# A hybrid decoder trunk: output projection interleaved with the last attention unit, last FFN sums moved to VectorE, forget gates one tile later

## The chip, the core and the metric

The kernel runs on one core of a Trainium2 chip. That core has a matrix engine (TensorE, PE in the profile; its weight loads are PEld), three engines for elementwise work (VectorE or DVE, ScalarE or ACT, GpSimd or POOL), a queue engine that issues the DMAs (SyncE or SP), an on-chip memory of 128 partitions (SBUF), and an accumulator memory for TensorE's results (PSUM, eight banks of 128x512 f32). The metric is device time in microseconds (us), the lower the better.

## What is computed

Two decoder layers on 1024 tokens of width 1024, all in f32. Layer 0 has sparse attention (compressed, selected and windowed keys, mixed by gates), layer 1 has full attention with forget gates; both add attention into 256 memory tokens, one output projection, and a gated FFN with a causal convolution of width 3. Cut to what matters here:

```python
for l in range(2):
    h = rms_norm(x, attn_norm[l])
    if l == 0:
        o_mix, q_mem = nsa_mixer(h, ...)             # 12 heads: compressed + selected + window
    else:
        hs = rms_norm(x, kv_norm) @ w_kv_shared       # k, v and 12 forget columns
        log_f = log_sigmoid(hs[..., 2 * MIX_W:] + b_fgate)
        dcum = cumsum(log_f, axis=1)                  # enters the scores of layer 1
        o_mix = forgetting_attention(q, k_sh, v_sh, dcum)
    o_mem = memory_attention(q_mem, mem, ...)         # 4 heads
    x = x + concat([o_mix, o_mem]) @ w_o[l]           # the output projection
    x = x + conv_ffn(rms_norm(x, ffn_norm[l]), ...)   # up, conv, silu(a) * b, down
return rms_norm(x, final_norm)
```

## The kernel before

**Arithmetic.** Every f32 product is made of three matmuls of halves: `mm3` (L157, L158, L159) multiplies high by high, high by low and low by high. `split` makes the halves of an operand: ScalarE rounds the high half (L81), VectorE subtracts it from the source (L82).

**Attention** (`attention`). The work is cut into units, one head (`h`) and one half of the tokens (`c`), and each unit into steps `k`. A step transposes a block of probabilities on TensorE (`turn_p`, L399), splits it into `pt` (ScalarE L406, VectorE L409) and two steps later multiplies it by the values (`value`, L422). Scores of later units are begun between the steps (`begin`, L300), masked and maximised on VectorE (L330), exponentiated on ScalarE (L343) and scaled on GpSimd (`normalise`, L366). In layer 0 a unit has a selected part (`ps`), a windowed part (`pw`) and a compressed part (`pc`). A finished unit's result goes through `ob` to DRAM (L515); when both heads of a pair are there, `operand` reads the block back (`wr<-o`, L480), adds the two halves on GpSimd (L481) and splits it into `hT`, the left operand of the output projection. There is one operand for each `c` and each of eight blocks `kt`; block 5 (heads 10 and 11) is the last. At the first step of the last unit the kernel also loads and splits the left half of `w_o` (`load_block`, L190, four pieces of 512 KB through a ring of three `wr` buffers).

**Output projection** (`out_proj`). For each half `n` of the columns and each of eight token tiles `t`, 24 matmuls accumulate in one PSUM bank (`psb`, four banks), with block 5 last; VectorE adds the bank to the residual `x` (L871), which is loaded from DRAM right behind the attention (L1124).

**FFN.** `Up.run` writes out by hand, slot by slot, the order in which VectorE and ScalarE work. `left(k)` makes four sums of two hidden tiles on GpSimd (L1408 to L1411) for the down projection, `store(k)` writes seven tiles of sums to DRAM (`gd`, L1417). `Down.step` multiplies: each step is twelve matmuls; its left operand is read back with `wr<-gd` (`fetch`, L1508), and both operands are split (`prep`) into a ring of four `wh`/`wl` pairs, up to three steps ahead. `sums` (L1529 to L1533) prepares weights on VectorE. `left(10)`, the last, stands behind the first `Down` steps; it writes into `ws` tiles.

**Forget gates.** In `middle`, eight tiles of `layer1_v` (24 matmuls of 390 columns each) are computed in a loop over `t`; the generator `forget` is advanced between them. Its first piece is a chain of small VectorE operations (L994 to L1003), its second multiplies the result by two triangular matrices on TensorE (L1008, L1009), its third transposes and stores (`dd`, L1026).

**Order.** Every engine executes its own queue strictly in order, and all DMAs stand in one queue, SP's. Outside of the stretches that are ordered by hand, a scheduler places the instructions in each queue when the program is built; the places below are read from the built programs.

Of the kernel before, what the change touches and what calls it, by code (L numbers as in the profile page):

```python
# [17 lines left out]
P = 128  # L18
D = 1024
S = 1024  # L20
NT = S // P
KT = D // P
CH = 512
# [6 lines left out]
NF = DFF // P  # L30
# [12 lines left out]
class Trunk:  # L43
# [398 lines left out]
    def attention(self, ap, l, od, units, work, spare, lead=4, lag=2, lead_work=2):  # L442

        units = list(units)
        steps, items, users = [], [], {}
        for k, u in enumerate(units):
            u["start"] = len(steps)
            steps += self.value_steps(u)  # L450
        ends = {id(q[0]): k for k, st in enumerate(steps) for q in st["ps"]}
        for k, u in enumerate(units):
            its, brs = [], u["branches"]
            for br in brs:
                tag, _, bufs = br["p"]
                same = users.setdefault(tag, [])
                br["early"] = ends[id(same[-bufs])] if len(same) >= bufs else -10 ** 9
                same.append(br)
            scored = brs if len(brs) == 1 else brs[0:2]
            for i, br in enumerate(scored):  # L460
                early = max(b["early"] for b in (br, br.get("joint", br)))
                due = next(k for k in range(u["start"], len(steps)) if any(q[0] is br for q in steps[k]["ps"])) - lead
                gs = self.groups(br)
                its += [{"u": u, "br": br, "grp": g, "first": j == 0, "last": g is gs[-1], "early": early, "due": due} for j, g in enumerate(gs)]
                its[-1]["norm"] = (i, len(brs) if br is scored[-1] else i + 1)
            its[0]["load"] = True
            items += its
        self.pace(steps, items)
        n_fill = units[-spare]["start"] if spare else len(steps)
        total, owed, done = sum(n for _, n, _ in work), 0.0, set()  # L470
        work = [[name, gen] for name, _, gen in work]
        later, halves, whole, oT = {}, [], [], []

        def operand():

            if not oT:
                oT.extend(self.hpair() for _ in range(2))
            c, kt = whole.pop(0)
            raw = self.wraw([P, 2, CH])
            self.nc.sync.dma_start(raw, od[c][:, kt * P:(kt + 1) * P, :].rearrange("s p q -> p s q"))  # L480
            self.nc.gpsimd.tensor_tensor(raw[:, 0], raw[:, 0], raw[:, 1], ALU.add)  # L481
            self.split(raw[:, 0], oT[c][0][:, kt, :], oT[c][1][:, kt, :])

        def after(k, slot, f):
            later.setdefault((k, slot), []).append(f)

        def run(k, slot):
            for f in later.pop((k, slot), ()):
                f()

        def advance():
            nonlocal total
            total -= 1
            if next(work[0][1], 0) == 0:
                done.add(work.pop(0)[0])

        def begin(k, it):
            if "load" in it:
                while not set(it["u"]["needs"]) <= done:
                    advance()  # L500
                it["u"]["load"]()
            self.score(it)
            after(k + 1, "max", lambda: self.maximum(ap, it))
            after(k + 1, "exp", lambda: self.exponent(ap, it))
            if "norm" in it:
                after(k + 2, "norm", lambda: self.normalise(ap, it["u"], *it["norm"]))

        def finish(k, u):
            h, c = u["at"]

            def out():
                ot = self.sb(ap, [P, CH], F32, "ob", 2)
                self.nc.scalar.activation(ot, u["o"], AF.Copy)
                for i in range(2):
                    self.nc.sync.dma_start(od[c][i, h * HD:(h + 1) * HD, :], ot[i * HD:(i + 1) * HD, :])  # L515
                halves.append((c, h // 2))
                if halves.count((c, h // 2)) == 2:
                    whole.append((c, h // 2))
            after(k + 1, "exp", out)

        first = min(it["at"] for it in items)
        for k in range(first, len(steps) + lag + 4):
            st = steps[k] if 0 <= k < len(steps) else None
            run(k, "max")
            if st:
                self.turn_p(ap, st)
            run(k, "exp")
            if st:
                self.lower_p(st)
            run(k, "norm")  # L530
            while items and items[0]["at"] <= k:
                begin(k, items.pop(0))
            if k < 0 and lead_work and items:
                for _ in range(lead_work):
                    if work:
                        advance()
            if st and k < n_fill:
                owed += max(total, 0) / (n_fill - k)
                while owed >= 1 and work:
                    owed -= 1  # L540
                    advance()
            if 0 <= k - lag < len(steps):
                self.value(steps[k - lag])
                if steps[k - lag]["end"]:
                    finish(k, steps[k - lag]["u"])
            if not work and whole and k % 4 == 0:
                operand()
            if k == units[-1]["start"]:
                w_o = self.load_block(self.a["w_o"][l], [(0, CH)])
        while whole:  # L550
            operand()
        assert not work and not later
        return oT, w_o

    @staticmethod
    def causal(c, mask):
# [291 lines left out]
    def out_proj(self, l, oT, pool, fx, up):  # L848

        nc, a = self.nc, self.a
        (oT, w), B, late, gb = oT, up.B, [], None
        for n in range(2):
            if n:
                w = self.load_block(a["w_o"][l], [(CH, CH)])
                gb = self.wraw([P, D])
                nc.sync.dma_start(gb, a["ffn_norm"][l:l + 1, :].to_broadcast([P, D]))
                up.load(0)
            for t in range(NT):  # L860
                ps = self.psb()
                oh, ol = oT[t // 4]
                o = (t % 4) * P
                for kt in (0, 1, 2, 3, 4, 6, 7, 5):
                    self.mm3(ps, (oh[:, kt, o:o + P], ol[:, kt, o:o + P]), w(kt, 0, CH), kt == 0, kt == 5)
                if n == 0 and t == NT - 1:
                    up.conv_turn()
                if n and t == NT - 1:
                    up.split_a(0)
                xs = self.x[:, t, n * CH:(n + 1) * CH]  # L870
                nc.vector.tensor_tensor(xs, ps, xs, ALU.add)  # L871
                turns, late = late, self.norm_part(pool, fx, l, t, gb, B) if n else []
                if n and t in (2, 4):
                    (up.sums_21 if t == 2 else up.sums_34)(0)
                if n and t == 1:
                    turns, late = [], turns + late
                for f in turns:
                    f()
        up.load(1)
        up.first(0)  # L880
        up.second(0, True)
        late[0]()
        up.split_a(1)
        up.split_21(0)
        up.first(1)
        for f in late[1:]:
            f()
        up.take_early(0)
        up.second(1, True)
        up.take_early(1)  # L890
        for i in range(4):
            self.turn_split(self.x[:, 4 + i, CH:], B["t3"], i)
            self.turn_split(self.x[:, i, CH:], B["t4"], i)
            if i == 1:
                up.third(0)
                up.split_34(0)
                up.split_b(0)
                up.sums_21(1)
                up.sums_34(1)
# [259 lines left out]
    def middle(self, oT):  # L1159
# [4 lines left out]
        with tc.tile_pool(name="fx0", bufs=1) as fx:  # L1164
            down = self.gated(0, oT, a["x"][0], fx)
            with tc.tile_pool(name="l1v", bufs=1) as vp:
# [25 lines left out]
                with tc.tile_pool(name="l1w", bufs=1) as wp:  # L1192
# [2 lines left out]
                        self.layer1_v(vp, h, 0, t, got["w"], self.psb()[:, 0:390], fb, z)  # L1195
                    forget = self.forget(wp, z)
                    for t in range(NT):
                        if t % 2 == 0:
                            next(forget, None)
                        self.layer1_v(vp, h, 1, t, w1, self.psb()[:, 0:390], fb, z)  # L1200
        return h, got["g"]
# [29 lines left out]
class Up:  # L1231
# [167 lines left out]
    def left(self, k):  # L1399
# [4 lines left out]
        else:  # L1404
            two = [self.k.sb(self.pool, [P, 2, CH], F32, "ws", 2) for _ in range(2)]
            s1, s2, s4 = two[0][:, 0], two[0][:, 1], two[1][:, 0]
        add = self.k.nc.gpsimd.tensor_tensor
        add(s1, g[:, CH:], h[:, CH:], ALU.add)  # L1408
        add(s2, s1, g[:, :CH], ALU.subtract)
        add(g[:, CH:], g[:, :CH], g[:, CH:], ALU.subtract)  # L1410
# [212 lines left out]
```

## Time and profile before

| | |
|---|---|
| time, median of 3 runs (lowest to highest) | 2561.35 us (2555.23 to 2565.48) |
| the profiled execution: its time, its span | 2560.4 us, 2558.4 us |
| granted TensorE clock, mean | 0.993 |
| busy: PE, PEld, DVE, ACT, POOL | 96%, 80%, 73%, 53%, 30% |
| read from and written to HBM | 139 GB/s over the span |

The span goes from the first to the last instruction of the program; what the time has beyond it, 2 us, lies around it. Times in the rows are microseconds from the start of the span. A row of a timeline has the start, the duration, engine, line, operation, tiles and shapes, and in brackets how long the engine had been idle before it and what ended that. In the names of the program's order, the numbers behind a name tell buffers apart; in the profile's rows they are left out.

### The profile page before, as it was taken

The page shows a single profiled execution, that of the slowest core. Times are in us where ns is not written, and L with a number is a line of the kernel's source. Part 1 is how long each engine was busy: PE and PEld are TensorE (multiplying, and loading weights), DVE is VectorE, ACT ScalarE, POOL GpSimd, SP SyncE. Part 2 cuts the span into 40 slices and gives each one's busy share as a digit, 9 for nine tenths or more (in the row PEclk, how much of TensorE's full clock was granted, in tenths as well). Part 3 has the DMA queues.
Part 4 walks back from the last instruction along what each step waited for, and adds up shares of the span by engine and source line. Part 5 has one row for each costly group of instructions (what it writes and reads, how often), then busy time and mean ns, then how long its engine had stood idle before and what let it go on. Part 6 is the DMA issues. An engine that isn't in the chain of part 4 may idle for free.

```text
span 2558.4 us, 35716 instructions
## 1 busy us (share of the span) xinstructions
PE 2460.7 (96%) x12306; PEld 2052.7 (80%) x12306; DVE 1868.4 (73%) x3180; ACT 1345.1 (53%) x2565; POOL 764.1 (30%) x620
## 2 busy tenths in 40 slices
PE   7898999988999999999999999999999999999998
PEld 7787877776878888887888988887777888888787
DVE  5758888887377787777765467878476778878766
ACT  5337777876244454444454356767235444444444
POOL 0104444544034555543000000000234455454000
PEclk9999999999999999999999999999999999999999
DMA  8473234344423333357334466665622233337623
GB/s 251 141 217 113 66 86 116 105 117 131 149 79 102 100 112 99 101 178 280 100 124 149 150 188 189 194 185 169 217 106 86 95 104 111 99 100 263 206 91 123
DMA packets 303276, 357.68 MB, mean 140 GB/s; under 512 B 38024, under 2 KB 183288, under 8 KB 303096
## 3 DMA queue, kind: packets, MB, share of 16 engines
q1 hardware_dynamic: 303096, 355.41, 44.2%
q8 instruction: 97, 1.59, 0.3%
q14 instruction: 83, 0.68, 0.1%
HBM read 245.55 MB, written 109.78 MB: 139 GB/s over the span
## 4 chain that ended last, share of the span: by engine, by line
PE 73%; DVE 8%; ACT 6%; DMA 5%; issue 3%; POOL 3%; SPq 1%; POOLq 0%; ACTq 0%; DVEq 0%
PE psa L157 11%; PE psa L158 11%; PE psa L159 11%; PE psb L157 9%; PE psb L159 9%; PE psb L158 9%; PE psb L399 4%; PE psa L300 4%; PE psb L422 4%; DVE pt L409 2%; POOL ws L1408 2%; ACT pt L406 1%; DMA hT<-in_w_down_dram 1%; DVE ps L330 1%; DVE wl L82 1%
## 5 line engine op out<-in xcount | busy, mean ns | idle before, releaser
L81 ACT ACTIVATE wh<-wr 128x512 fp32r<-128x512 f32 (+2 forms) x254 | 192.7, 763 | 336.4 <-PE psb L159 141.6
L82 DVE TENSOR_TENSOR wl<-wr,wh 128x512 fp32r<-128x512 f32 (+2 forms) x254 | 242.1, 957 | 151.1 <-ACT wh L81 150.4
L1389 DVE SCALAR_TENSOR_TENSOR v<-u,cw,v 128x1023 f32<-128x1023 f32 (+1 forms) x176 | 271.7, 1544 | 69.0 <-ACT v L1387 68.8
L409 DVE TENSOR_TENSOR pt<-psb,pt 128x512 fp32r<-128x512 f32 (+2 forms) x380 | 246.8, 659 | 66.5 <-ACT pt L406 63.4
L1387 ACT ACTIVATE v<-u,cw 128x1024 f32<-128x1024 f32 x88 | 109.6, 1246 | 310.3 <-DVE u L1376 283.6
L406 ACT ACTIVATE pt<-psb 128x512 fp32r<-128x512 f32 (+2 forms) x380 | 213.3, 572 | 87.6 <-PE psb L399 81.3
L422 PE MATMUL psb<-pt,vv 128*128 128x512 f32 (+2 forms) x864 | 225.7, 356 | 18.5 <-DVE pt L409 12.8
L159 PE MATMUL psa<-hT,wl 128*128 128x512 f32 x560 | 218.0, 389 | 0.8 <-DVE wl L82 0.8
L157 PE MATMUL psa<-hT,wh 128*128 128x512 f32 x560 | 218.4, 391 | 0.0
L158 PE MATMUL psa<-hT,wh 128*128 128x512 f32 x560 | 217.9, 389 | 0.0
L300 PE MATMUL psa<-kk,qq 128*128 128x512 f32 (+4 forms) x792 | 184.7, 347 | 13.9 <-DVE stat L330 6.9
L121 POOL TENSOR_TENSOR rs<-ss,consts 128x1 f32<-128x1 f32 x40 | 22.8, 570 | 555.5 <-DVE ss L119 347.5
L422 PEld LDWEIGHTS psb<-pt,vv 128*128 128x128 f32 x864 | 141.0, 191 | 43.9 <-DVE pt L409 21.1
L343 ACT ACTIVATE ps<-ps,stat 128x128 f32<-128x128 f32 (+1 forms) x192 | 147.8, 771 | 46.6 <-DVE stat L330 46.3
L481 POOL TENSOR_TENSOR wr<-wr 128x512 f32<-128x512 f32 x32 | 42.0, 1318 | 428.0 <-ACT pt L406 243.7
L157 PE MATMUL psb<-hT,wh 128*128 128x512 f32 x384 | 156.7, 408 | 1.0 <-DVE pt L409 0.9
L399 PE MATMUL psb<-consts,ps 128*128 128x128 f32 x928 | 148.4, 277 | 8.1 <-DVE pt L409 3.3
L159 PE MATMUL psb<-hT,wl 128*128 128x512 f32 x384 | 151.4, 394 | 0.0
L158 PE MATMUL psb<-hT,wh 128*128 128x512 f32 x384 | 150.7, 393 | 0.0
L330 DVE CUSTOM_DVE_ANT_0 ps<-psa,caub 128x128 f32<-128x128 f32 (+1 forms) x192 | 138.9, 750 | 15.2 <-PE psa L300 14.9
L300 PEld LDWEIGHTS psa<-kk,qq 128*128 128x128 f32 x792 | 120.3, 191 | 30.3 <-DVE stat L330 10.3
L157 PE MATMUL psa<-hx,wh 128*128 128x512 f32 x368 | 144.0, 392 | 0.4 <-ACT u L1379 0.4
(300 smaller groups left out, 6759.3 us busy)
## 6 DMA issues: line engine op xcount, KB each, us to landing
wr<-in_w_up_dram SPq DMA_DIRECT2D x88, 512.0 KB
wr<-gd SPq DMA_DIRECT2D x154, 256.0 KB
gd<-v SPq DMA_DIRECT2D x88, 256.0 KB
o<-ob SPq DMA_DIRECT2D x128, 128.0 KB
wr<-o SPq DMA_DIRECT2D x32, 512.0 KB
hT<-in_w_down_dram SPq DMA_DIRECT2D x64, 256.0 KB
gd<-gs SPq DMA_DIRECT2D x60, 256.0 KB
qd<-st SPq DMA_DIRECT2D x56, 256.0 KB
```

The lines of the kernel that those rows point to most:

```text
L81: nc.scalar.activation(hi, src, AF.Copy)
L82: nc.vector.tensor_tensor(lo, src, f32(hi), ALU.subtract)
L157: mm(out, lh, rh, start=first, stop=False, skip_group_check=more)
L158: mm(out, lh, rl, start=False, stop=False, skip_group_check=more)
L159: mm(out, ll, rh, start=False, stop=last, skip_group_check=more)
L300: nc.tensor.matmul(out, w, rhs, start=b not in banks[:i], stop=b not in banks[i + 1:])
L330: self.nc.vector.tensor_tensor_reduce(p, s, br["spans"][ii][2], -1.0, 3e38, ALU.add, ALU.min, br["stat"][:, 0, ii:ii + 1])
L399: nc.tensor.transpose(tp[0:kb, x:x + P], br["pt"][ii][:, o:o + kb], self.ident)
L406: nc.scalar.activation(st["hi"], st["src"], AF.Copy)
L409: self.nc.vector.tensor_tensor(st["lo"], st["src"], f32(st["hi"]), ALU.subtract)
L422: self.nc.tensor.matmul(out, v, t, start=st["begin"] and i == 0, stop=st["end"] and i == len(mms) - 1)
L1389: nc.vector.scalar_tensor_tensor(v[:, d:], u[:, :S - d], cw[:, tap, i:i + 1], v[:, d:], ALU.mult, ALU.add)
```

## The change

It has three parts.

1. In layer 0 the left half of `w_o` is loaded eight steps earlier (`early`). From the last unit on, when all scores have been begun, each step also issues up to two pieces of the output projection (`ahead`, `out_part`): a piece is three matmuls for one token tile and one block. Seven blocks of the first four token tiles go into four banks of the two `psa` buffers, in the order 0, 1, 2, 3, 6, 4, 7, each as soon as its operand stands in the program's order. `out_proj` then does the seven blocks of tiles 4 and 5, and block 5 of tiles 0 to 5, before tiles 6 and 7. Layer 1 keeps the old way.
2. The four sums of `left(10)`, in both layers, are made on VectorE instead of GpSimd.
3. `forget` is advanced ahead of the tiles 0, 3 and 5 instead of 0, 2, 4 and 6.

```diff
@@ attention
+        early = units[-1]["start"] - 8 if l == 0 else units[-1]["start"]
+        made, rows = set(), {}
...
             self.split(raw[:, 0], oT[c][0][:, kt, :], oT[c][1][:, kt, :])
+            made.add((c, kt))
+
+        def ahead():
+
+            for kt in (0, 1, 2, 3, 6, 4, 7):
+                for t in range(4):
+                    while (0, kt) not in made:
+                        yield
+                    if not rows:
+                        rows.update(enumerate(p[:, x * CH:(x + 1) * CH] for p in (self.psa(), self.psa()) for x in range(2)))
+                    self.out_part(rows[t], oT[0], w_o, t, kt, kt == 0, False)
+                    yield
...
-            if k == units[-1]["start"]:
+            if k == early:
                 w_o = self.load_block(self.a["w_o"][l], [(0, CH)])
+                part = ahead()
+            if l == 0 and k > early + 8 and not items:
+                for _ in range(2):
+                    next(part, None)
         while whole:
             operand()
+        if l == 0:
+            for _ in part:
+                pass
...
+    def out_part(self, ps, oT, w, t, kt, first, last):
+        oh, ol = oT
+        o = (t % 4) * P
+        self.mm3(ps, (oh[:, kt, o:o + P], ol[:, kt, o:o + P]), w(kt, 0, CH), first, last)
@@ out_proj
-            for t in range(NT):
-                ps = self.psb()
...
-                for kt in (0, 1, 2, 3, 4, 6, 7, 5):
+            most = (0, 1, 2, 3, 4, 6, 7)
+            parts = [(t, most + (5,)) for t in range(NT)]
+            if n == 0 and rows:
+                parts = [(t, (5,)) for t in range(4)] + [(4, most), (5, most), (4, (5,)), (5, (5,))] + parts[6:]
+            open_ = dict(rows) if n == 0 else {}
+            for t, kts in parts:
+                ps = open_.setdefault(t, None) or self.psb()
+                open_[t] = ps
+                for kt in kts:
+                    self.out_part(ps, oT[t // 4], w, t, kt, kt == 0, kt == 5)
+                if kts[-1] != 5:
+                    continue
@@ middle
-                        if t % 2 == 0:
+                        if t in (0, 3, 5):
                             next(forget, None)
@@ Up.left
-        add = self.k.nc.gpsimd.tensor_tensor
+        add = (self.k.nc.gpsimd if k < NF // 2 - 1 else self.k.nc.vector).tensor_tensor
```

Three places of the built programs matter below. The first is VectorE's queue shortly before the last unit of layer 0: `wl` is the low half of `w_o`, `hT` an operand of the output projection, `pt` a step's block of probabilities, `stat` the sums of the unit whose `ps` GpSimd scales next (the reciprocal is L355). Before:

```order
L354 TENSOR_SCALAR stat_6814<-stat_6814 128x4
L330 ISA pw_1185_6931,stat_6814<-psa_6923,winb 128x640
L330 ISA stat_6814 128x1
L409 TENSOR_TENSOR pt_6910<-psb_6905,pt_6910 128x512
L355 RECIPROCAL stat_6814<-stat_6814 128x4
L330 ISA pc_6932,stat_6814<-psa_6923,cmpb 128x64
L330 ISA stat_6814 128x1
L82 TENSOR_TENSOR wl_7082<-wr_7079,wh_7081 128x1024
L409 TENSOR_TENSOR pt_6940<-psb_6935,pt_6940 128x512
```

After:

```order
L409 TENSOR_TENSOR pt_6910<-psb_6905,pt_6910 128x512
L82 TENSOR_TENSOR wl_6940<-wr_6937,wh_6939 128x1024
L354 TENSOR_SCALAR stat_6814<-stat_6814 128x4
L82 TENSOR_TENSOR wl_6946<-wr_6943,wh_6945 128x1024
L355 RECIPROCAL stat_6814<-stat_6814 128x4
L82 TENSOR_TENSOR wl_6952<-wr_6949,wh_6951 128x1024
L330 ISA pw_1197_6955,stat_6814<-psa_6923,winb 128x640
L330 ISA stat_6814 128x1
```

Three of the four `wl` now stand together around the reciprocal, and the next step's `pt` (`pt_6964`, in the place of `pt_6940`) stands behind them; further on, `hT_6057<-wr_6971` stands ahead of `pt_7003`, the third block of probabilities from here, where before no operand stood.

The second is GpSimd's queue at the same place: `ps_1163` and the last `pw` are the probabilities of the last unit, `wr` the operands that it adds. Before:

```order
L366 TENSOR_SCALAR ps_1163_6815<-ps_1163_6815,stat_6814,gates 128x1024
L366 TENSOR_SCALAR pw_1185_6931<-pw_1185_6931,stat_6814,gates 128x640 x4
L360 TENSOR_TENSOR stat_6814<-stat_6814,gates 128x4
L481 TENSOR_TENSOR wr_7112<-wr_7112 128x512
L362 TENSOR_TENSOR pc_6932<-pc_6932,stat_6814 128x256
```

After:

```order
L366 TENSOR_SCALAR ps_1163_6815<-ps_1163_6815,stat_6814,gates 128x1024
L483 TENSOR_TENSOR wr_6971<-wr_6971 128x512
L483 TENSOR_TENSOR wr_7051<-wr_7051 128x512
L483 TENSOR_TENSOR wr_7112<-wr_7112 128x512
L483 TENSOR_TENSOR wr_7188<-wr_7188 128x512
L366 TENSOR_SCALAR pw_1197_6955<-pw_1197_6955,stat_6814,gates 128x640 x4
```

Two adds that stood ahead of the last unit's `ps` before, and two that stood behind its `pw`, now stand between them.

The third is VectorE's queue behind `left(10)` in layer 0; each pair of `wl` belongs to one step of `Down`, and L1396 is the slots' work before it. Before:

```order
L1396 TENSOR_TENSOR v_11178<-v_11178,v_11213 128x1024
L82 TENSOR_TENSOR wl_11275<-wr_11102,wh_11274 128x512
L82 TENSOR_TENSOR wl_11275<-hx_10966,wh_11274 128x512
L82 TENSOR_TENSOR wl_11299<-wr_11102,wh_11298 128x512
L82 TENSOR_TENSOR wl_11299<-hx_10966,wh_11298 128x512
```

After:

```order
L82 TENSOR_TENSOR wl_11273<-hx_10964,wh_11272 128x512
L1440 TENSOR_TENSOR ws_11290<-v_11046,v_11176 128x512
L1561 TENSOR_TENSOR hx_11003<-hT_11120 128x512
L1441 TENSOR_TENSOR ws_11290<-ws_11290,v_11046 128x512
L1442 TENSOR_TENSOR v_11046<-v_11046 128x512
L1443 TENSOR_TENSOR ws_11291<-v_11176,ws_11290 128x512
L82 TENSOR_TENSOR wl_11297<-wr_11100,wh_11296 128x512
```

The four sums and one of the weights' sums stand between two steps' pairs.

More of the change, by code (lines that the diff above doesn't have):

```diff
@@ L547, in attention @@
                 operand()
-            if k == units[-1]["start"]:
+            if k == early:
                 w_o = self.load_block(self.a["w_o"][l], [(0, CH)])
+                part = ahead()
+            if l == 0 and k > early + 8 and not items:
+                for _ in range(2):
+                    next(part, None)
         while whole:
             operand()
+        if l == 0:
+            for _ in part:
+                pass
         assert not work and not later
-        return oT, w_o
+        return oT, w_o, rows
+    def out_part(self, ps, oT, w, t, kt, first, last):
+        oh, ol = oT
+        o = (t % 4) * P
+        self.mm3(ps, (oh[:, kt, o:o + P], ol[:, kt, o:o + P]), w(kt, 0, CH), first, last)
     @staticmethod
@@ L852, in out_proj @@
         nc, a = self.nc, self.a
-        (oT, w), B, late, gb = oT, up.B, [], None
+        (oT, w, rows), B, late, gb = oT, up.B, [], None
         for n in range(2):
@@ L859, in out_proj @@
                 up.load(0)
-            for t in range(NT):
-                ps = self.psb()
-                oh, ol = oT[t // 4]
-                o = (t % 4) * P
-                for kt in (0, 1, 2, 3, 4, 6, 7, 5):
-                    self.mm3(ps, (oh[:, kt, o:o + P], ol[:, kt, o:o + P]), w(kt, 0, CH), kt == 0, kt == 5)
+            most = (0, 1, 2, 3, 4, 6, 7)
[10 more added lines that the diff above has]
+                    continue
                 if n == 0 and t == NT - 1:
```

## The prediction

> **What bounds the kernel now.** I read the page's busy times first, then the chain that ended last, then every wait of TensorE over 2 us, then the rows around those that the change touches. The forecast is made against the profiled execution, 2560.4 us (span 2558.4, 2 us around it); the median of the runs, 2561.35, is 0.04% above it.
>
> ```profile
> PE 2460.7 (96%) x12306; PEld 2052.7 (80%) x12306; DVE 1868.4 (73%) x3180; ACT 1345.1 (53%) x2565; POOL 764.1 (30%) x620
> PE 73%; DVE 8%; ACT 6%; DMA 5%; issue 3%; POOL 3%; SPq 1%; POOLq 0%; ACTq 0%; DVEq 0%
> ```
>
> TensorE is busy for 96% of the span and makes up 73% of the chain. The change removes no matmul, so it can only win where TensorE waits, or where its clock drops behind a wait. GpSimd's 3% on the chain is odd for an engine busy 30% of the time, and the chain through layer 0's FFN shows it:
>
> ```profile
> 1166.45 20.27 POOL ws L1408
> 1189.36 0.32 SPq L1417
> 1191.24 3.78 DMA wr<-gd
> 1195.12 1.16 ACT wh L81 x2
> ```
>
> One add of `left(10)` takes 20.27 us; the stores of its sums leave after it; the read-back lies behind them; ScalarE splits what arrives; and TensorE stands still until then. Windows of the stretch (columns: busy time and count of PE, PEld, DVE, ACT, POOL, then granted clock, DMA share, GB/s):
>
> ```profile
> 1140.00:1160.00 20.00, 20.00 (x88) 16.05 (x87) 15.77 (x18) 10.62 (x16) 1.25 (x1) 1.00 1.03 373
> 1160.00:1180.00 20.00, 20.00 (x90) 16.54 (x89) 20.00 (x31) 10.47 (x19) 13.55 (x1) 1.00 0.80 294
> 1180.00:1200.00 20.00, 16.49 (x65) 12.88 (x64) 9.79 (x17) 5.85 (x11) 10.50 (x4) 0.88 0.53 192
> ```
>
> VectorE is busy for all of 1160 to 1180, just where the add crawls. TensorE's rows, layer 0 and then layer 1:
>
> ```profile
> 1191.76 0.39 PE L159 MATMUL psa<-wh,wl 128*128 128x512 f32 x1
> 1192.44 0.39 PE L159 MATMUL psa<-wh,wl 128*128 128x512 f32 x1
> 1196.32 0.79 PE L157 MATMUL psa<-wh 128*128 128x512 f32 x1 [3.49 <-ACT wh L81]
> 1202.33 0.40 PE L158 MATMUL psa<-wl,wh 128*128 128x512 f32 x1
> 2370.12 0.39 PE L159 MATMUL psa<-wh,wl 128*128 128x512 f32 x1
> 2373.55 0.79 PE L157 MATMUL psa<-wh 128*128 128x512 f32 x1 [3.04 <-ACT wh L81]
> 2379.96 0.39 PE L159 MATMUL psa<-wh,wl 128*128 128x512 f32 x1
> ```
>
> A matmul here normally starts every (1192.44 − 1191.76) / 3 = 0.227 us. Behind each wait the clock is halved for 13 or 14 matmuls.
>
> **Part 2, the last sums on VectorE.** Removed: the wait and its slow clock. In layer 0 the stretch 1192.44 to 1202.33 holds 14 starts: 9.89 − 14 × 0.227 = 6.7 us too long. In layer 1, 2370.12 to 2379.96 holds 15: 9.84 − 15 × 0.227 = 6.4. Added: four VectorE operations a layer. Their place and their price:
>
> ```profile
> 1157.52 0.40 PE L158 MATMUL psb<-wl,wh 128*128 128x512 f32 x1
> 1167.42 0.68 DVE L82 TENSOR_TENSOR wl<-wr,wh 128x512 fp32r<-128x512 f32 x1
> 1168.63 0.68 DVE L1529 TENSOR_TENSOR hx<-hT 128x512 f32<-128x512 f32 x1
> 1171.14 1.01 SPq L1417 DMA_DIRECT2D gd<-v  x2
> 1195.78 0.69 DVE L82 TENSOR_TENSOR wl<-wr,wh 128x512 fp32r<-128x512 f32 x1 [10.21 <-ACT wh L81]
> ```
>
> L1529 is an add of the same shape: 0.68, or 0.60 from start to start. The order puts the four and one L1529 between the pairs of two steps: 5 × 0.6 = 3.0, so the pair that began at 1167.42 begins at 1170.4 and ends at 1171.6. A step is 12 × 0.227 = 2.72 us; with `Down`'s first at 1157.5, the pair is needed at 1157.5 + 6 × 2.72 = 1173.8: 2.2 us in hand where there were 5.2. The cover behind it is VectorE's idle 10.21 us; without that cover it would cost 4 × 0.68 = 2.7 a layer. The seven stores can then leave from 1171.1, the first two already did, 7 × 0.43 (the pace of 1.01 for two, rounded down) to 1174.2; with the chain's 3.78 the read-back lands at 1178, while ScalarE's last splits before the gap end about 1183. The wait goes wholly: −6.7 and −6.4. Next in line is the DMA: 1140 to 1160 ran at a share of 1.03, and anything fetched late there would be seen next.
>
> The Trainium skill's page "SBUF — State Buffer", section "Who interferes with whom", says that VectorE and GpSimd share one port pair, held exclusively for a whole instruction, and that only VectorE work on the shared pair shuts GpSimd out. The trace agrees in direction, and goes past "one instruction": 20.27 us over some 31 back-to-back instructions of about 0.68. By that rule the whole 6.7 goes as well.
>
> **Part 3, later forget gates.** TensorE now stops in front of the triangular matmuls until VectorE's chain is done:
>
> ```profile
> 1422.24 0.34 PE L159 MATMUL psb<-bh,hT 128*128 128x390 f32 x1
> 1424.84 0.25 DVE L1003 SCALAR_TENSOR_TENSOR lsg<-lsg 128x96 f32<-128x96 f32 x1
> 1425.19 0.43 PE L1008 MATMUL psb<-lsg,tri 128*128 128x96 f32 x2 [2.60 <-issue]
> 1437.76 1.60 SPq L1026 DMA_DIRECT2D dd<-drow  x4
> 1465.18 0.39 SPq L1079 DMA_DIRECT2D ky<-dd  x1
> ```
>
> A 390-column matmul starts every 0.18, so the gap is 1425.19 − 1422.42 = 2.77. One tile more in front is 24 × 0.18 = 4.3 us, longer than the gap: −2.8. The transposes and the four `dd` stores come 4.3 later; the first reader is issued 27 us behind them, which covers it. At 2.60 us idle the clock stayed up.
>
> **Part 1, output projection between the last unit's steps.** Filled are TensorE's waits in the last unit:
>
> ```profile
> 614.84 0.83 PE L422 MATMUL psb<-pt,vv 128*128 128x512 f32 x2 [0.73 <-ACT ob L513]
> 617.37 0.50 PE L422 MATMUL psb<-pt,vv 128*128 128x512 f32 x1 [1.02 <-DVE pt L409]
> 621.77 0.50 PE L422 MATMUL psb<-pt,vv 128*128 128x512 f32 x1 [1.66 <-ACT pt L406]
> 623.57 0.50 PE L422 MATMUL psb<-pt,vv 128*128 128x512 f32 x1 [1.30 <-DVE pt L409]
> 620.61 0.63 ACT L81 ACTIVATE hT<-wr 128x512 fp32r<-128x512 f32 x1 [3.87 <-POOL wr L481]
> 614.76 4.42 POOL L366 TENSOR_SCALAR pw<-pw,stat,gates 128x640 f32<-128x640 f32 x4 [7.17 <-DVE stat L355]
> ```
>
> 0.73 + 1.02 + 1.66 + 1.30 = 4.7. The largest come from an operand's add that stood behind a `pw` scaling of 4.42 and held ScalarE 3.87. The 84 matmuls of the pieces are moved work, 19.1 us, not added.
>
> But the load of `w_o` and the operands move too, and they land in a tight place, ahead of the first piece:
>
> ```profile
> 602.18 0.17 DVE L355 RECIPROCAL stat<-stat 128x4 f32<-128x4 f32 x1
> 602.38 1.22 DVE L82 TENSOR_TENSOR wl<-wr,wh 128x1024 fp32r<-128x1024 f32 x1
> 602.55 5.05 POOL L366 TENSOR_SCALAR ps<-ps,stat,gates 128x640 f32<-128x640 f32 x4 [4.20 <-DVE stat L330]
> 606.90 0.69 DVE L409 TENSOR_TENSOR pt<-psb,pt 128x512 fp32r<-128x512 f32 x1 [0.34 <-ACT pt L406]
> ```
>
> In the new order two of the `wl` stand ahead of the reciprocal, two scans now behind it: it moves from 602.2 to about 603.9, and the `ps` scaling with it, to 604.3 + 5.05 = 609.3. Behind that on GpSimd stands the add of `wr_6971`, 1.26 (its fellow ended ScalarE's wait); ScalarE's `hT` 0.63 stands ahead of the blocks that feed TensorE, VectorE's `hT` 0.68 ahead of `pt_7003`, 0.69: its value matmul can start at 612.6, where the third block's ended at 606.90 + 0.69 = 607.6 before. That is 5.0 late, and nothing can fill it, since the first piece needs operands that wait behind the same scaling. Net: 5.0 − 4.7 = +0.3.
>
> The delay comes in two waits of about 2.5 each, the first behind three `wl` ahead of `pt_6964`. An idle time of 2.60 cost no clock, 3.04 cost 6.4 − 3.0 = 3.4 and 3.49 cost 3.2. Two such waits cost between 0 and 6.6; 2.5 is nearest to the row without loss, but with little room, so I take +1.5. The Trainium skill, "TensorE: Matmul & The Clock Gate", section "What's actually happening", gives about 3.4 us of idling before the clock drops; here 3.04 already did, so the measurement decides, and by the page alone the term would be 0.
>
> Behind the attention:
>
> ```profile
> 640.32 0.69 DVE L82 TENSOR_TENSOR hT<-wr,hT 128x512 fp32r<-128x512 f32 x1 [10.01 <-ACT hT L81]
> 641.54 31.06 SPq L190 DMA_DIRECT2D wr<-in_w_o_dram  x4
> 669.88 1.06 ACT L81 ACTIVATE wh<-wr 128x1024 fp32r<-128x1024 f32 x1 [29.60 <-PE psb L159]
> ```
>
> The last operand arrived with some 10 us of other work beside it; 57 matmuls, 12.9 us, now stand ahead of its use. The last attention matmul comes about 16 us later (72 of the 84 stand ahead of it), and so do the loads of `x` (4 MB) and of the right half of `w_o`: 641.5 + 16, with 5.5 MB at 373 GB/s from about 653 done at 667.5. ScalarE wants it at 669.9. Covered by 2 us; at 294 GB/s it would be 2 late. I take 0.
>
> **Sum.** −6.7 − 6.4 − 2.8 + 0.3 + 1.5 = −14.1; 2560.4 − 14.1 = 2546.3, say 2546. A measurement of this kernel can tell about 0.5%, 13 us; the forecast lies just beyond that.
>
> **Rivals.**
> - The interleaving works and nothing in it stalls: −6.7 − 6.4 − 2.8 − 4.7 = −20.6, 2539.8. For it: ScalarE's 3.87 has its cause removed. Against it: the place of the adds in GpSimd's queue.
> - VectorE becomes the bound in `Down`, as 20.00 of 20 busy suggests: 2 × 2.7 given back, 2551.7. Against it: 10.21 idle right behind.
> - Both waits of part 1 lose the clock, and the second pair of operands holds ScalarE again for about 3: 2546.3 + 6.6 − 1.5 at the most, near 2551.
> - The change doesn't do what it says, since the read-back is late for another reason than GpSimd's add: only part 3 and part 1 remain, −2.8 + 1.8, 2559.
> - Slower: in the last unit and the projection's first half (603 to 660, with frequent short waits) TensorE runs at half clock throughout. Each us of work then costs one more, some 50 in all: about 2595. It decides once more than 14 + 13 = 27 us stay slow. Against it: the clock came back within 6 us behind both waits above.
>
> **How the numbers follow.** Forecast 0.42 (its own range 2543 to 2549), no stall 0.25, both clocks lost 0.15, VectorE bound 0.10, no effect 0.05, slower 0.03. The range 2538 to 2555 holds the first four with the bounds of the clock term and leaves out the last two and the tails. Faster by over 0.5% is under 2548: most of the forecast's case, 0.34, the no-stall case, 0.25, and a little of the rest, 0.60 in all; within 0.5% 0.37; slower 0.03.
>
> **What the changed profile would show.** Right: no wait over 1 us and clock 1.00 in `Down` behind `left(10)` in both layers, the sums on VectorE at 0.6 to 0.7 each; no wait at L1008; two waits of 2 to 3 us in the last unit behind `pt` and `hT`, a GpSimd add of an operand ending near 610.6. Wrong: the `wh` wait near 1192 still there or moved to VectorE's pairs, a clock below 1.00 in 600 to 660, a wait of ScalarE for `w_o` at the projection's second half, or a last unit without any wait.

## The result, and the profile after

The changed kernel takes 2546.36 us (median of 6 runs, 2541.75 to 2549.29) against 2561.11 us before (6 runs, 2555.23 to 2565.48): 14.75 us less by the medians, a ratio of 0.9937 with a 95% interval of 0.9923 to 0.9951, or 16 us less (12.5 to 19.7). The forecast was 2546. Its profiled execution is the longest of the six (2549.29 us); its span is 2547.5 us, 10.9 less than before's.

From the page, busy times and the chain by engine:

```profile
PE 2457.8 (96%) x12306; PEld 2053.2 (81%) x12306; DVE 1881.0 (74%) x3188; ACT 1347.9 (53%) x2565; POOL 715.9 (28%) x612
PE 79%; DVE 7%; ACT 6%; issue 3%; DMA 3%; POOL 1%; SPq 0%; POOLq 0%; ACTq 0%; DVEq 0%
```

GpSimd is down from 3% to 1% of the chain, and its busy time by 48 us for eight adds fewer. Layer 0's `Down`, windows and then rows of VectorE and of SP's queue:

```profile
1160.00:1180.00 20.00, 20.00 (x90) 16.55 (x89) 19.95 (x30) 11.54 (x19) 0.00 (x0) 1.00 1.04 385
1180.00:1200.00 20.00, 20.00 (x90) 16.57 (x89) 20.00 (x34) 8.46 (x15) 0.00 (x0) 1.00 0.82 277
```

```profile
1170.10 0.69 DVE L1440 TENSOR_TENSOR ws<-v,v 128x512 f32<-128x512 f32 x1
1172.51 0.69 DVE L1443 TENSOR_TENSOR ws<-v,ws 128x512 f32<-128x512 f32 x1
1173.11 0.69 DVE L82 TENSOR_TENSOR wl<-wr,wh 128x512 fp32r<-128x512 f32 x1
1179.33 7.93 SPq L1540 DMA_DIRECT2D wr<-gd  x6
```

TensorE has no idle time left and the clock is 1.00. The first sum took 20.27 us and takes 0.69; the next pair of `wl` begins at 1173.11; the read-back is issued at 1179.33 instead of 1191.24. In `middle`, the last step of the forget chain is done 1.6 us before TensorE comes to the triangular matmuls, and no idle time stands there:

```profile
1420.79 0.25 DVE L1035 SCALAR_TENSOR_TENSOR lsg<-lsg 128x96 f32<-128x96 f32 x1
1422.67 0.35 PE L1040 MATMUL psb<-lsg,tri 128*128 128x96 f32 x2
```

Part 1 is less clean. Ahead of the first piece (621.28), GpSimd, ScalarE, TensorE and the clock:

```profile
607.89 4.87 POOL L366 TENSOR_SCALAR ps<-ps,stat,gates 128x640 f32<-128x640 f32 x4 [5.31 <-ACT pt L406]
612.74 2.50 POOL L483 TENSOR_TENSOR wr<-wr 128x512 f32<-128x512 f32 x2
614.04 0.63 ACT L81 ACTIVATE hT<-wr 128x512 fp32r<-128x512 f32 x1 [2.92 <-POOL wr L483]
615.21 0.44 PE L399 MATMUL psb<-consts,ps 128*128 128x128 f32 x2 [1.62 <-ACT ob L527]
```

```profile
605.00:610.00 5.00, 3.34 (x18) 2.17 (x18) 4.77 (x10) 4.25 (x9) 2.10 (x2) 0.97 0.71 198
610.00:615.00 5.00, 3.59 (x12) 2.75 (x12) 1.92 (x5) 2.08 (x6) 5.00 (x5) 0.69 0.34 118
615.00:620.00 5.00, 4.58 (x20) 3.81 (x21) 5.00 (x14) 4.44 (x11) 0.23 (x1) 0.66 0.67 161
```

The `ps` scaling comes late, the operand's add stands behind it, ScalarE stands still for 2.92 us for it, TensorE runs dry, and the clock is at two thirds for 10 us. That is the stall of the forecast, in another shape: not two waits of about 2.5, but several short ones (0.53, 0.81, 0.46, 0.39) and this one, 1.62 here and 3.14 in e3, e6 and e8. From the first piece on TensorE has no wait in the rest of the projection's first half, and none at the right half of `w_o`, whose loads the forecast took as covered.

The spans of two executions can't tell a microsecond, but the stretches can. For the table, TensorE's instruction at the same place of the program was found in both traces and its start compared with that in the trace of before; the numbers are how much longer (+) or shorter (−) a stretch became, in us. Stretches are named by their times before.

| profile of | 550–588 (untouched) | 588–690 (part 1) | 1150–1240 (part 2) | 1410–1447 (part 3) | 1780–1870 (untouched) | 2340–2385 (part 2) |
|---|---|---|---|---|---|---|
| changed kernel | +3.3 | −1.1 | −6.7 | −2.8 | +3.2 | −6.5 |
| the same, again (c_after) | 0.0 | −0.4 | −6.8 | −2.8 | +2.4 | −6.5 |
| e1: part 2 alone | 0.0 | +1.1 | −6.8 | 0.0 | +2.4 | −6.5 |
| e2: part 3 alone | 0.0 | −0.1 | −0.2 | −2.8 | −0.3 | +0.1 |
| e3: part 1 alone | 0.0 | −1.4 | −1.1 | +1.6 | +1.0 | −0.8 |
| e4: parts 2 and 3 | +3.1 | +1.2 | −6.8 | −2.8 | +3.5 | −6.5 |
| e5: first sum only | +2.6 | +2.6 | −1.7 | 0.0 | +1.1 | −2.2 |
| e6: load only | 0.0 | +1.9 | −0.7 | +1.6 | +1.7 | −1.1 |
| e7: operands' adds on VectorE, layer 0 | 0.0 | −4.1 | −6.7 | −2.8 | +2.7 | −6.5 |
| e8: eight more adds on VectorE | 0.0 | −1.5 | +2.2 | −2.8 | +3.4 | +1.7 |
| e9: as e7, both layers | +3.2 | −4.0 | −6.8 | −2.8 | −2.2 | −6.5 |
| e10: as e9, all adds | +2.0 | −4.4 | −6.8 | −2.8 | −1.3 | −6.5 |

Where a kernel leaves a stretch alone, its entry shows how far executions differ: up to 1.1 in the stretches of part 2, 1.6 in that of part 3, and from −0.3 to +3.5 in the untouched ones.

### The profile page after: what moved, and what is told of

The parts are those of the page before. It is cut to its first block, busy times and chain, and to the rows that moved or that the text cites. A ratio compares the mean times of both kernels' runs of the same rounds, so it can differ in the third digit from the quotient of the medians.

```text
span 2547.5 us, 35696 instructions
## 1 busy us (share of the span) xinstructions
PE 2457.8 (96%) x12306; PEld 2053.2 (81%) x12306; DVE 1881.0 (74%) x3188; ACT 1347.9 (53%) x2565; POOL 715.9 (28%) x612
## 4 chain that ended last, share of the span: by engine, by line
PE 79%; DVE 7%; ACT 6%; issue 3%; DMA 3%; POOL 1%; SPq 0%; POOLq 0%; ACTq 0%; DVEq 0%
PE psa L157 13%; PE psa L158 13%; PE psa L159 13%; PE psb L157 10%; PE psb L159 10%; PE psb L158 9%; PE psb L399 4%; PE psb L422 4%; PE psa L300 4%; DVE pt L409 2%; ACT pt L406 2%; ACT ps L343 1%; DVE ps L330 1%; PE psb L937 1%; ACT wh L81 1%
## 5 line engine op out<-in xcount | busy, mean ns | idle before, releaser
L1421 DVE SCALAR_TENSOR_TENSOR v<-u,cw,v 128x1023 f32<-128x1023 f32 (+1 forms) x176 | 280.1, 1592 | 68.7 <-ACT v L1419 68.5
L422 PE MATMUL psb<-pt,vv 128*128 128x512 f32 (+2 forms) x864 | 224.3, 355 | 14.9 <-DVE pt L409 10.9
L157 PE MATMUL psa<-hT,wh 128*128 128x512 f32 x560 | 218.4, 391 | 0.0
L157 PE MATMUL psb<-hT,wh 128*128 128x512 f32 x384 | 157.4, 410 | 1.1 <-DVE pt L409 0.9
L157 PE MATMUL psa<-hx,wh 128*128 128x512 f32 x368 | 144.1, 392 | 0.5 <-ACT u L1411 0.5
```

Source lines behind the costliest of these rows:

```text
L157: mm(out, lh, rh, start=first, stop=False, skip_group_check=more)
L422: self.nc.tensor.matmul(out, v, t, start=st["begin"] and i == 0, stop=st["end"] and i == len(mms) - 1)
L1421: nc.vector.scalar_tensor_tensor(v[:, d:], u[:, :S - d], cw[:, tap, i:i + 1], v[:, d:], ALU.mult, ALU.add)
```

## The experiments

**One part at a time.** Each kernel is before with some of the diff's hunks: e1 the one line in `Up.left`, e2 the one line in `middle`, e4 both, e3 all the others.

```diff
 e1, e4
-        add = self.k.nc.gpsimd.tensor_tensor
+        add = (self.k.nc.gpsimd if k < NF // 2 - 1 else self.k.nc.vector).tensor_tensor
 e2, e4
-                        if t % 2 == 0:
+                        if t in (0, 3, 5):
```

> The kernel before with part 2 alone. Theory (GpSimd's add crawls behind VectorE and the stores wait for it): both Down waits go, 6.7 + 6.4 = 13.1 us less, near 2548, and nothing elsewhere. Rival (VectorE is the bound in Down, so its four added sums are paid): the waits go but 2.7 us a layer come back, 7.7 less, near 2553.4. Rival (the read-back is late for another reason): no change.

> The kernel before with part 3 alone. Theory: the 2.8 us gap before the triangular matmuls goes and nothing takes its place, 2558.3. Rival (the later gates delay their first reader in layer 1's attention): no gain, 2561. The difference is near what timing can tell; the trace decides, by a wait before the triangular matmuls and by the times of the rows before and behind the eight tiles.

> The kernel before with part 1 alone. Theory on record: +0.3 from delay against filled waits, +1.5 from the clock, so about +1.8, 2563. Rival (the changed kernel's trace: TensorE's start times against before gain 1.1 us between the last units and the end of the projection's first half): -1.1, 2560. In both the last unit shows ScalarE waiting some 3 us for GpSimd's add of an operand and a granted clock near 0.7 for some 10 us.

> Parts 2 and 3 without part 1. If part 1 costs 1.8 us, this is faster than all three parts by that much: 13.1 + 2.8 = 15.9 less than before, near 2545. If part 1 gains 1.1 us, it is slower than all three by that, near 2547.5. Either way within 2 us of the changed kernel's 2546.4.

Measured, beside before at 2563.35: e1 2552.12 (ratio 0.9961, 0.9949 to 0.9973), e2 2561.05 (0.9994, 0.9984 to 1.0003), e3 2560.55 (0.9989, 0.9980 to 0.9997), e4 2550.67 (0.9951, 0.9939 to 0.9963). The three parts alone make −11.2, −2.3 and −2.8, together −16.3, so they add up within the intervals. e1's interval is −6.9 to −13.1, with the expected −13.1 at its edge; its trace has −6.8 and −6.5. Part 3 alone can't be told from no change by its timing; the trace shows its −2.8. Part 1 was expected between +1.8 and −1.1 and came out at −2.8 (−0.8 to −5.1): it gains. e4 was expected within 2 us of the changed kernel and is 4.3 above it, on the side that part 1 gains; but each was timed beside its own before, and by those it is 12.7 less and the changed kernel 14.75 less, 2.1 apart.

**Is it VectorE that slows GpSimd's add?** e5 is before with only the first of the four sums on VectorE.

```diff
-        add(s1, g[:, CH:], h[:, CH:], ALU.add)
+        one = (self.k.nc.gpsimd if k < NF // 2 - 1 else self.k.nc.vector).tensor_tensor
+        one(s1, g[:, CH:], h[:, CH:], ALU.add)
```

> The kernel before, with only the first of the four last sums on VectorE in both layers; the other three stay on GpSimd. Theory (any GpSimd add with VectorE's two-input work back to back beside it crawls): now the second sum takes some 17 us, until VectorE's run ends near 1186, and the waits of 3.5 and 3.0 us in TensorE stay: no gain, within 1 us of before. Rival (the first add crawls because of itself, its place or its operands): the other three take 1.3 us each, the waits go, 13.1 us less.

2560.55 beside 2562.66 (0.9991, 0.9978 to 1.0004): no gain that can be told. Now the second sum crawls, on GpSimd's rows of layer 0 and layer 1:

```profile
1174.41 18.46 POOL L1410 TENSOR_TENSOR ws<-ws,v 128x512 f32<-128x512 f32 x1 [27.03 <-DVE ws L1409]
1192.84 1.28 POOL L1411 TENSOR_TENSOR v<-v 128x512 f32<-128x512 f32 x1
2352.26 18.47 POOL L1410 TENSOR_TENSOR ws<-ws,v 128x512 f32<-128x512 f32 x1 [26.97 <-DVE ws L1409]
```

The last row of VectorE's run in layer 0:

```profile
1190.43 1.30 DVE L1532 TENSOR_TENSOR hx<-hx,hx 128x512 f32<-128x512 f32 x2
```

It isn't the first sum, nor its operands: in both kernels the add that starts while VectorE runs back to back lasts until that run ends, and the next takes 1.28. The run ends at 1191.73 and the add at 1192.87, 1.14 later; in layer 1, and in both layers of before, it is 1.15 or 1.16. The waits in TensorE shrink to 2.52 and 1.77: the run ends at the same point of the program as in before, and behind it GpSimd now has two adds left instead of three, 1.25 us less.

**Was there room for the sums?** e8 is the changed kernel with the first sum made nine times.

```diff
+        if k == NF // 2 - 1:
+            for _ in range(8):
+                add(s1, g[:, CH:], h[:, CH:], ALU.add)
```

> The changed kernel with eight more adds on VectorE ahead of the four sums in each layer (the first sum made nine times; the result is the same), 8 x 0.6 = 4.8 us. Theory on record (2.2 us in hand behind the sums): TensorE waits 4.8 - 2.1 = 2.7 us once in each layer, 5.4 more in all, and 3 more per layer if the clock drops behind it: 2552 to 2558. Rival (the 10 us of VectorE's idle time before were the true cover, so VectorE has room): no change. Rival (every VectorE operation here is on the path): 9.7 more, without a single wait.

2563.48 beside 2562.66 (1.0009, 0.9998 to 1.0020): the whole gain of part 2 is gone. TensorE, twice in layer 0 and once in layer 1, and the pair that the first wait is for:

```profile
1173.35 1.07 PE L157 MATMUL psb<-wh 128*128 128x512 f32 x4
1181.14 0.80 PE L158 MATMUL psb<-wl,wh 128*128 128x512 f32 x1 [5.45 <-DVE wl L82]
2360.24 0.79 PE L158 MATMUL psb<-wl,wh 128*128 128x512 f32 x1 [5.64 <-DVE wl L82]
1179.78 0.70 DVE L82 TENSOR_TENSOR wl<-wr,wh 128x512 fp32r<-128x512 f32 x1
```

The waits are twice what was expected, 2.7, because the order put a weights' sum behind each of the eight copies: 16 operations of 0.60, 9.6 us, lie ahead of the pair, not 4.8. The built order also pulls matmuls of `L157`, which don't need the pair, ahead of the one that does. Without them that one would have come 0.23 behind the first, at 1173.58; it starts at 1181.14, 7.6 late. So 9.6 − 7.6 = 2.0 was in hand, and the prediction had 2.2. The changed kernel's own rows agree: its pair ends at 1174.40, and the matmul that needs it starts 2.1 later:

```profile
1176.53 0.39 PE L158 MATMUL psb<-wl,wh 128*128 128x512 f32 x1
```

The stretch became 2.2 + 6.7 = 8.9 longer than in the changed kernel: 5.45, a wait of 0.54 just before it, and some 2.9 for the slow clock and the restart. That VectorE has 10 us of idle time behind it didn't help; the pair's due time decides.

**What do the load and the pieces of part 1 each do?** e6 is e3 without the two places that advance `ahead`.

```diff
-            if l == 0 and k > early + 8 and not items:
-                for _ in range(2):
-                    next(part, None)
...
-        if l == 0:
-            for _ in part:
-                pass
```

> Part 1 without its pieces: the left half of w_o is loaded and split eight steps earlier, the operands move with it, the output projection keeps its old order. Theory on record (the load and the operands' adds in their new place delay the last unit by 5 us, the pieces then win back what waits there are): TensorE's times between the last units and the end of the projection's first half grow by 3 to 5 us against before. Rival (the earlier load costs little, and the pieces win little): 0 to 1 us.

2565.20 beside 2562.66 (1.0009, 0.9999 to 1.0019); its stretch is 1.9 longer than before's. ScalarE and TensorE:

```profile
611.18 0.63 ACT L81 ACTIVATE hT<-wr 128x512 fp32r<-128x512 f32 x1 [2.91 <-POOL wr L483]
612.35 0.44 PE L399 MATMUL psb<-consts,ps 128*128 128x128 f32 x2 [3.14 <-ACT ob L527]
```

The delay belongs to the load and the operands behind it, as expected: at the last matmul ahead of where the first piece would stand, TensorE is 5.2 behind before. At the end of the stretch only 1.9 is left and not 3 to 5, since the old waits shrink: 0.73, 1.02, 1.66 and 1.30 in before; here the last two are 0.59 and 0.36, the first two are gone, and one of 0.53 is new. Whether they shrink because TensorE comes late to them or because the operands' adds no longer stand behind `pw` isn't separated. The pieces, with the new order of the projection, win 3.3 on top (+1.9 to −1.4 in e3).

**Can the stall be taken out?** e7 is the changed kernel with the operands' adds from the early load on, in layer 0, on VectorE.

```diff
-            self.nc.gpsimd.tensor_tensor(raw[:, 0], raw[:, 0], raw[:, 1], ALU.add)
+            eng = self.nc.vector if begun else self.nc.gpsimd
+            eng.tensor_tensor(raw[:, 0], raw[:, 0], raw[:, 1], ALU.add)
...
             if k == early:
+                begun.extend([1] if l == 0 else [])
```

> The changed kernel, with the operands' adds from the early load on (layer 0) on VectorE instead of GpSimd. Theory (ScalarE's wait of 2.9 us for an add that stands behind the ps scaling, and the slow clock behind it, are what part 1 loses): the wait goes, the clock stays at 1.00 between 600 and 625, and the stretch up to the end of the projection's first half is 3 to 5 us shorter than in the changed kernel: near 2542.5. Rival (VectorE is what bounds the last unit): six adds of 0.6 come on top, no gain or up to 3.6 more, 2546 to 2550.

2544.10 beside 2562.66 (0.9925, 0.9910 to 0.9940). The same windows as above:

```profile
610.00:615.00 5.00, 4.13 (x28) 3.42 (x28) 5.00 (x14) 3.98 (x10) 0.94 (x1) 1.00 0.70 178
615.00:620.00 5.00, 5.00 (x30) 3.99 (x29) 4.85 (x13) 3.96 (x9) 0.08 (x1) 1.00 0.29 89
```

The clock stays at 1.00, ScalarE's 2.9 is gone, and the stretch goes from −1.1 to −4.1: 3 us, the low end of what was expected. VectorE is full from 610 to 615, and TensorE waits for it there once, 0.87 at 611.76, so it bounds little. Ahead of the first piece TensorE is now 2.3 behind before, where the changed kernel is 5.3 behind. So the place of the adds behind the `ps` scaling, with the clock that dropped there, is shown to cost 3.0 of the 5.3; the other 2.3 stay.

**Layer 1 as well.** e9 drops the `if l == 0` of e7; c_after is the changed kernel again, beside it; e10 is e9 with all operands' adds of both layers on VectorE, those before the load too.

```diff
 e9
-                begun.extend([1] if l == 0 else [])
+                begun.append(1)
 e10
-            eng = self.nc.vector if begun else self.nc.gpsimd
+            eng = self.nc.vector
```

> The changed kernel once more, beside the next one. Theory (the executions differ by two places that the change does not touch: a tiny VectorE operation near 565 held by GpSimd's adds, 0 or 3.3 us, and the operands of layer 1's projection near 1810, 0 to 3.5 us): stretches of the change as before, -6.7, -2.8, -6.5 and about -1.3, and a time of 2541 to 2549 depending on those two. Rival (part 1's gain is chance): its stretch comes out at 0 or above.

> The changed kernel with the operands' adds from the load of w_o on in both layers on VectorE (0.6 each instead of GpSimd's 1.3). Theory (in layer 1 an operand's chain of load, add and two splits goes through three buffers, and TensorE waits 0.4 to 2.5 us for the last ones): 0.7 us less per operand shortens the chain, the waits at layer 1's projection go or shrink, 2 to 3 us less than with layer 0 alone, near 2541.5. Rival (the loads through the three buffers set the pace, not the add): no change from 2544.

> All operands' adds of both layers on VectorE, those before the load of w_o too (ten more than in the kernel before this). Theory (a VectorE operation of 0.17 us near 565 takes 0.46 or 3.47 in the profiles taken so far, until one or all of three GpSimd operations beside it have ended): without adds on GpSimd the 3.47 cannot come, and that stretch never loses its 2.6 to 3.3 us; on average 1 us less, against up to 10 x 0.6 more for VectorE where the attention waits for it: 2540 to 2546, with no 3.47 in its profile. Rival (VectorE is so full in layer 0's attention that the adds all count): 2547.

c_after 2546.92 (0.9934, 0.9921 to 0.9948) and e9 2541.11 (0.9913, 0.9900 to 0.9927), both beside 2562.89; e10 2541.62 beside 2562.60 (0.9912, 0.9894 to 0.9930). TensorE before two of the last operands of layer 1's projection, in the changed kernel and then in e9:

```profile
1807.98 0.50 PE L157 MATMUL psb<-wh,hT 128*128 128x512 f32 x1 [0.41 <-ACT hT L81]
1814.28 0.56 PE L157 MATMUL psb<-wh,hT 128*128 128x512 f32 x1 [2.33 <-ACT hT L81]
```

```profile
1806.23 0.50 PE L157 MATMUL psb<-wh,hT 128*128 128x512 f32 x1 [0.73 <-ACT hT L81]
```

e9's row is the one at 1807.98, where the wait grows to 0.73; at the place of the other, 2.33, it has no wait. The granted clock from 1810 to 1820 is 0.83 in the changed kernel and 1.00 in e9. The stretch turns from +3.2 and +2.4 to −2.2. e9 is the fastest version that was run, 5.8 us under the changed kernel beside it, layer 0's adds included; e10 gains nothing over it, and its first stretch is 2.0 longer all the same, against what was expected. c_after's part 1, −0.4, is short of the −1.3 expected but gains.

## Why the prediction was right, and where it was not

**Part 2, right in mechanism and size.** −6.7 and −6.4 were forecast; −6.7 or −6.8 and −6.5 stand in every profile that has it. The pair was to begin 3.0 later than before; its rows moved from 1167.42 to 1173.11, which is 5.7, of which 2.67 is the offset of the whole program there. One step on the way was off and cost nothing: the seven stores were to take 3.0, from a pace of 0.43 where the row said 0.5, and took 4.6, and the read-back was still early enough. The rival that VectorE bounds was wrong at four sums and right at twelve adds (e8). The Trainium skill's page "SBUF — State Buffer", section "Who interferes with whom", speaks of a lock for one instruction; e5's 18.46 us confirm that an add can be shut out for a whole run of them.

**Part 3, right.** −2.8 forecast, −2.8 in each trace; the stretch behind it, with the reader of `dd`, is unchanged (+0.1 up to 1600).

**Part 1, right in mechanism, wrong in sign.** The step "net: 5.0 − 4.7 = +0.3", with 1.5 for the clock, gave +1.8; the traces give −0.4 to −1.5, and e3's timing −2.8. The delay was placed well: ScalarE's `hT` was to start at 609.3 + 1.26 = 610.6, and at this program's offset there, 3.6, that is 614.2; it started at 614.04. Both sizes were off. Delay and clock together were to cost 6.5. At the last matmul ahead of the first piece, TensorE's lag behind before, counted from 588, is 5.3 in the changed kernel, 5.9 in c_after, 5.0 in e3 and 4.8 in e8. What is won back from there was to be 4.7, and is 6.3 or 6.4 in each of the four (5.3 + 1.1 in the changed kernel).

The 4.7 added the idle times in the brackets, and these understate a wait, because the profile lets a matmul end well behind the point where the next one normally starts: the one at 623.57 has a duration of 0.50. The waits at 621.77 and 623.57 start 1.80 apart, where such a pair normally takes 0.23: that is 1.57 lost, and the bracket says 1.30. So counted, the four waits cost 5.7 and not 4.7; the rest of the 6.3 isn't attributed. For parts 2 and 3 the prediction had counted from start to start, and there the sizes came out. e6 also shows that the pieces aren't all of what is won back: without them 3.3 of the 5.2 came back by itself.

In other executions the same waits cost more. In before they cost no clock, but 1.65 and 1.30 were followed by a slow clock in three of the five profiles without part 1. Windows of before and of e5:

```profile
625.00:630.00 5.00, 5.00 (x39) 4.50 (x37) 4.36 (x8) 3.31 (x7) 0.00 (x0) 1.00 0.00 0
```

```profile
625.00:630.00 5.00, 3.35 (x13) 2.85 (x14) 4.53 (x6) 2.50 (x5) 2.22 (x2) 0.61 0.14 51
```

(e1 has 0.82 there and e4 0.66.) Their stretches are 1.1, 1.2 and 2.6 longer than before's, whose own profile was among those that lost nothing. The mean without part 1 is +1.0, with it (changed kernel, c_after, e3, e8) −1.1, and the two groups don't overlap: part 1 is worth about −2.

**The sum.** Taken by its stretches, the change is worth −1.1 − 6.7 − 2.8 − 6.5 = −17.1 against before's profile, 3 more than the −14.1 of the forecast. That the median agrees to 0.4 us is partly chance: the changed kernel's profile loses 3.3 and 3.2 in two stretches that the change leaves alone, and what its other five runs lost there isn't known. Against before's median the ratio's interval, −12.5 to −19.7, holds both sums. The rival without a stall, −20.6, is what e7 comes near, −18.6 by its medians and −20.1 by its stretches, once the adds leave GpSimd.

## What to carry to other kernels

An add on GpSimd beside a full VectorE wasn't priced here by its usual duration but by when VectorE's run ended; on a path, four adds of 0.6 us in each layer on the busier engine were 13 us cheaper. A step that is put ahead of others takes its place in every queue: look on each engine for what it now stands behind, here an add behind a 5 us scaling, and move that piece first. Price a wait from start to start, not by the idle time in its brackets. And a stall that costs nothing more than itself in one profile can cost the clock in the next: price short waits from several executions.

## What the runs showed that was not expected

**VectorE can be held by GpSimd too.** In four of the twelve profiles of kernels that keep GpSimd's adds at 565 (all but e10), a 128x4 operation of VectorE that takes 0.17 elsewhere took 3.47 or 3.48; in the other eight 0.45 to 0.47. In the changed kernel, VectorE, GpSimd and TensorE:

```profile
564.96 3.48 DVE L354 TENSOR_SCALAR stat<-stat 128x4 f32<-128x4 f32 x1
565.93 2.48 POOL L483 TENSOR_TENSOR wr<-wr 128x512 f32<-128x512 f32 x2
568.71 0.92 PE L300 MATMUL psa<-kk,qq 128*128 128x512 f32 x2 [2.84 <-DVE stat L355]
```

It ends at 568.44, as GpSimd's last add does (565.93 + 2.48 = 568.41). In before it ends at 564.92, as GpSimd's first add does at 564.90. The four profiles are those whose first stretch in the table is 2.6 to 3.3 longer. Without adds on GpSimd (e10) the operation at that place took 0.17, though that stretch is 2.0 longer there, for a cause that isn't known. Why it is let in after one GpSimd operation in some executions and after four in a row in others stays open.

**The length of a wait alone doesn't decide the clock.** The 2.60 before the triangular matmuls cost nothing in before, e1 and e5, and 1.6 us in e3, with the same row; 2.62 in e6 cost 1.6 too:

```profile
1423.01 0.43 PE L1040 MATMUL psb<-lsg,tri 128*128 128x96 f32 x2 [2.60 <-issue]
```

```profile
1425.00:1430.00 5.00, 5.00 (x22) 5.00 (x22) 0.59 (x3) 0.38 (x1) 0.00 (x0) 0.72 0.42 106
```

In e5's layer 1 a wait of 1.77 and one of 0.31 were followed by half speed some 2 us later. The Trainium skill, "TensorE: Matmul & The Clock Gate", section "What's actually happening", gives an idle window of about 3.4 us; here shorter waits lost the clock in some executions and not in others.
